# Delta-rule block inverses on 64 by 64 quarters of TensorE, and the sequences' states on column tiles and halves of rows

## The chip, the core and the metric

The kernel runs on one core of a Trainium2 chip. The metric is the device time of one execution in microseconds, taken as the median of the runs shown. One execution was taken by the hardware profiler; its trace is what the rows further down are read from. The engines are TensorE (PE; its weight loads are listed as PEld), VectorE (DVE), ScalarE (ACT), GpSimd (POOL) and SyncE (SP), which issues most DMAs.

## What is computed

One inference step of a two-layer decoder trunk: a gated delta-rule layer, then a sparse-attention layer, each followed by a convolutional feed-forward block. There are 512 new prompt tokens and 8 decoding sequences of 4 tokens each, width 1024. The change touches only the delta rule's core of the first layer. In the reference, cut to what matters (8 heads, key and value width 128):

```python
decay = jnp.exp(jnp.where(tril, G[..., :, None] - G[..., None, :], NEG))
kk = jnp.einsum('bhncd,bhnsd->bhncs', k, k)
A = jnp.where(strict, beta[..., :, None] * kk * decay, 0.0)
T = lax.linalg.triangular_solve(eye + A, eye, left_side=True, lower=True, unit_diagonal=True)
u_v = T @ (v * beta[..., None])
w_k = T @ (k * (beta * jnp.exp(G))[..., None])
def step(S, xs):                      # over the chunks of a sequence
    u = uvc - wkc @ S
    o = (qc * jnp.exp(Gc)[..., None]) @ S + qkc @ u
    S = S * jnp.exp(glc)[..., None, None] + jnp.einsum('bhcd,bhce->bhde', kdc, u)
    return S, o
```

The prompt is worked on in chunks; for each the inverse of a unit triangular matrix is wanted. The decoding sequences bring their own states S, two heads times eight sequences in a group.

## The kernel before

The kernel is written against a scheduling layer: each engine's instructions are put in order by the layer from the program's order and its own estimate of when operands are there, and tiles are recycled from pools with a fixed number of buffers. `gdn_core` holds the section of the change. It mixes generators: `run` takes several streams with a weight each, and `attend` always advances the stream that is furthest behind by its weight, so the `yield` values of a stream set how its operations are interleaved with the others'.

The prompt's eight heads go in two halves of four, `B[0]` and `B[1]`, over four chunks of 128 tokens: `gdn_blocks` (the matrix `na` per head, 128 by 512: four chunks side by side), `gdn_small` (the inverses of 16 by 16 diagonal blocks, on VectorE), `gdn_prep`, `gdn_inverse` (16 by 16 blocks merged to 32, 64 and 128), `gdn_scan` (the chunks in order, with the state) and `gdn_result`. The decode groups run beside them, four calls of `gdn_decode` cut into slices by `part(n)`.

`gdn_inverse` starts from Y, the block-diagonal inverses laid out by GpSimd (line 833). For each level it does three steps for each of the four heads of a half: four 128x128 transposes of Y into PSUM (line 840) and ScalarE's copy to X (line 841); four 128x128 matmuls of `na` and Y (line 847) and VectorE's product with the level's mask into R (line 849); four matmuls of X and R (line 857) and VectorE's subtraction from Y (line 858). All work on full 128-wide chunks at each level, and the mask leaves only the blocks of that level.

`gdn_decode` has, in its order: transposes and small matmuls for the group's 64 tokens (lines 938 to 989, most on 64x64), sixteen accumulated 128x128 matmuls of the spread keys and queries `zk` with the sixteen states (line 1001), the update u (line 1008) and the output (line 1013), and the new states: for each of four quarters of the states GpSimd spreads u (line 1033), a matmul with 64 rows of `kd` and 512 columns (line 1037), and VectorE's addition to the state (line 1039). `S0` is one buffer, so a group's states are loaded after the group before has stored its own.

The mask tile `cm` is loaded by a DMA that ScalarE issues at the head of the section (line 657); GpSimd clears `zk` after it in program order (line 658).

## Time and profile before

| what | value |
|---|---|
| median of three runs | 2026.49 us (2019.98 to 2029.86) |
| profiled execution, its own time | 2023.65 us |
| its span, first to last instruction | 2022.0 us |
| busy TensorE, share of the span | 1913.4 us, 95% |
| busy VectorE, ScalarE, GpSimd | 1138.1, 793.0, 602.6 us |
| mean granted TensorE clock | 0.966 of full |
| the section of the change | about 215 to 430 us from the span's start |

In a row of a timeline "x16" means sixteen consecutive instructions put together, and its length reaches from the first one's start to the last one's end; consecutive rows of TensorE overlap, since its instructions are pipelined. "128*128 128x128" is the shape of the stationary tile (rows by columns) and of the moving operand. A float32 matmul stands as two instructions (passes), a transpose as one. The name list is output, then inputs. "[0.20 <-PE ps L857]" tells how long the engine was idle before the row and what ended the wait.

### The profile page before, as it was taken

What the parts mean: (1) busy time and instruction counts of PE and PEld (TensorE: products, weight loads), DVE (VectorE), ACT (ScalarE), POOL (GpSimd) and SP (SyncE); (2) the same over time, 40 slices, a digit from 0 to 9 for tenths busy, and PEclk for the clock granted to TensorE, in tenths of its full rate; (3) what the DMA queues carried; (4) which work ended last, traced back from release to release, by engine and by line L of the source; (5) the groups of instructions that cost most, each with busy time, mean ns of one, the idle gap of its engine ahead of it and who ended that gap; (6) DMA issues with size and microseconds to landing.
All of it is one profiled execution on the core that took longest, in us unless ns stands there. A gap on an engine that the chain in (4) does not pass through costs nothing.

```text
span 2022.0 us, 42933 instructions
## 1 busy us (share of the span) xinstructions
PE 1913.4 (95%) x16796; PEld 1756.5 (87%) x16796; DVE 1138.1 (56%) x2215; ACT 793.0 (39%) x1517; POOL 602.6 (30%) x1164
## 2 busy tenths in 40 slices
PE   7999999989999999989989697999997999999997
PEld 7999878879999999989978374676776999999997
DVE  6675586665755655553330024676665476564654
ACT  5543335443433333342210003665754443342335
POOL 2332445112423322301334211233332243241321
PEclk9999989989999999999999787999998999999999
DMA  5222012142222232265578637687576222223221
GB/s 166 87 89 87 11 45 62 42 143 91 80 90 87 84 97 83 76 188 159 170 218 246 190 118 238 193 251 216 171 220 133 91 85 85 84 86 103 77 83 59
DMA packets 225647, 247.07 MB, mean 122 GB/s; under 512 B 29862, under 2 KB 181334, under 8 KB 225188
## 3 DMA queue, kind: packets, MB, share of 16 engines
q1 hardware_dynamic: 196564, 200.09, 32.7%
q10 hardware_dynamic: 19824, 24.72, 4.2%
q0 software_dynamic: 9056, 19.51, 3.3%
q8 instruction: 132, 2.16, 0.4%
q14 instruction: 71, 0.58, 0.1%
HBM read 211.38 MB, written 32.86 MB: 121 GB/s over the span
## 4 chain that ended last, share of the span: by engine, by line
PE 85%; DMA 6%; DVE 4%; ACT 2%; issue 1%; SPq 1%; POOL 0%; ACTq 0%; DVEq 0%; POOLq 0%
PE pdn L424 59%; PE ps L1523 6%; PE po L1825 2%; DMA kv<-in_cache_sel 1%; PE ps L1936 1%; PE pp L1805 1%; PE ps L1924 1%; PE pos L1995 1%; PE ps L847 1%; PE pp L1780 1%; PE ps L857 1%; DMA od<-od 1%; PE pq L1037 1%; PE pp L1781 1%; PE pq L1001 1%
## 5 line engine op out<-in xcount | busy, mean ns | idle before, releaser
L424 PE MATMUL pdn<-hh,whi 128*128 128x272 f32 (+1 forms) x2272 | 477.3, 291 | 3.1 <-ACT hh L323 2.3
L424 PE MATMUL pdn<-hh,wlo 128*128 128x272 f32 (+1 forms) x2272 | 472.1, 289 | 0.0
L424 PE MATMUL pdn<-hl,whi 128*128 128x272 f32 (+1 forms) x2272 | 470.1, 288 | 0.0
L397 ACT CAST whi<-wraw 128x1024 fp32r<-128x1024 f32 (+3 forms) x222 | 214.2, 966 | 454.1 <-PE pdn L424 393.4
L424 PEld LDWEIGHTS pdn<-hh,whi 128*128 128x128 f32 (+1 forms) x2272 | 357.4, 188 | 6.0 <-ACT hh L323 2.7
L424 PEld LDWEIGHTS pdn<-hl,whi 128*128 128x128 f32 (+1 forms) x2272 | 356.7, 188 | 0.7
L424 PEld LDWEIGHTS pdn<-hh,wlo 128*128 128x128 f32 (+1 forms) x2272 | 354.6, 188 | 1.1 <-issue 0.4
L398 DVE TENSOR_TENSOR wlo<-wraw,whi 128x1024 fp32r<-128x1024 f32 (+3 forms) x222 | 250.7, 1130 | 34.7 <-ACT whi L397 27.6
L1133 DVE SCALAR_TENSOR_TENSOR facc<-fext,par,facc 128x592 f32<-128x592 f32 x176 | 146.2, 831 | 19.5 <-ACT facc L1131 16.7
L453 DVE TENSOR_TENSOR xT<-pdn,xT 128x544 f32<-128x544 f32 x80 | 57.7, 724 | 163.9 <-PE pdn L424 163.9
L1126 POOL COPY fext<-fext 128x32 f32<-128x32 f32 x88 | 31.1, 353 | 393.1 <-DVE fext L1123 392.6
L424 PE MATMUL pdn<-gh,whi 128*128 128x272 f32 x704 | 146.3, 289 | 0.2
L424 PE MATMUL pdn<-gh,wlo 128*128 128x272 f32 x704 | 145.2, 288 | 0.3 <-DVE wlo L398 0.3
L424 PE MATMUL pdn<-gl,whi 128*128 128x272 f32 x704 | 144.9, 288 | 0.0
L1523 PE MATMUL ps<-x,wc 64*64 64x128 f32 (+1 forms) x2048 | 135.9, 401 | 7.9 <-DVE cT L1535 5.6
L1523 PEld LDWEIGHTS ps<-x,wc 64*64 64x64 f32 x2048 | 106.6, 155 | 37.1 <-issue 8.4
L1123 DVE TENSOR_TENSOR fext<-pdn,rstd 128x544 f32<-128x544 f32 x88 | 63.6, 725 | 114.0 <-PE pdn L424 113.3
L424 PEld LDWEIGHTS pdn<-gl,whi 128*128 128x128 f32 x704 | 110.0, 188 | 0.3 <-DVE gl L1147 0.2
L424 PEld LDWEIGHTS pdn<-gh,wlo 128*128 128x128 f32 x704 | 109.6, 188 | 0.8 <-DVE wlo L398 0.8
L424 PEld LDWEIGHTS pdn<-gh,whi 128*128 128x128 f32 x704 | 109.4, 188 | 0.8 <-ACT whi L397 0.7
L1790 POOL TENSOR_SCALAR e<-e,sm 128x128 f32<-128x128 f32 (+3 forms) x128 | 66.5, 540 | 110.1 <-DVE sm L1787 38.2
L1131 ACT ACTIVATE facc<-fext,par 128x592 f32<-128x592 f32 x88 | 77.6, 883 | 41.5 <-POOL fext L1126 41.4
(543 smaller groups left out, 3271.1 us busy)
## 6 DMA issues: line engine op xcount, KB each, us to landing
wraw<-in_ffn_w_up SPq DMA_DIRECT2D x40, 1024.0 KB
kv<-in_cache_sel SPq DMA_DIRECT2D x128, 256.0 KB
x<-in_cache_cmp SPq DMA_DIRECT2D x128, 128.0 KB
wraw<-in_gdn_w_in SPq DMA_DIRECT2D x15, 1024.0 KB
wraw<-in_ffn_w_down SPq DMA_DIRECT2D x16, 768.0 KB
x<-in_cache_cmp POOLq DMA_DIRECT2D x96, 128.0 KB, 3.4
wraw<-in_ffn_w_down SPq DMA_DIRECT2D x16, 640.0 KB
kv<-in_state_win SPq DMA_DIRECT2D x16, 512.0 KB
```

The costliest lines, as they stand in the source:

```text
L397: nc.scalar.copy(h, raw)
L398: nc.vector.tensor_tensor(l, raw, h.bitcast(F32), op=OP.subtract)
L424: nc.tensor.matmul(p[:mw, j, :TH], w[:, k, :mw], (x[k] if type(x) is list else x[:, k, :])[:, j * TH:(j + 1) * TH], start=k == 0 and n == ...
L453: self.nc.vector.tensor_tensor(self.two(self.xT[:, m, :]), p, self.two(self.xT[:, m, :]), op=OP.add)
L847: nc.tensor.matmul(p[:, s], B['na'][h][:, s], Y[h][:, s], start=True, stop=True)
L1123: nc.vector.tensor_tensor(self.two(ext[:, 2:2 + T]), p, self.two(rstd), op=OP.mult)
L1126: nc.gpsimd.tensor_copy(se[:, :, 2:6], ext[:, 514:546].rearrange("p (b j) -> p b j", j=4))
L1131: nc.scalar.activation(acc, ext[:, 0:592], AF.Identity, scale=ws[0], bias=self.pcol(f'ffn_b{i}', ft))
L1133: nc.vector.scalar_tensor_tensor(acc, ext[:, j:592 + j], ws[j], acc, op0=OP.mult, op1=OP.add)
L1523: nc.tensor.matmul(p[par][half(f), :n], W[c][half(par), d, :], x[half(par), :n, d], start=k == 0, stop=k == 31)
L1790: nc.gpsimd.tensor_scalar(ee, ee, sm[:, qt:qt + 1], 1.0, op0=OP.mult, op1=OP.mult)
L1825: nc.tensor.matmul(po[:, kt * 128:], vw, part[:, poff[kt]:poff[kt] + w], start=br == 0 and kt == 0 and part is ph, stop=br == 1 and kt == ...
```

## The change

In `gdn_inverse` the levels 16 and 32 work on the two diagonal 64 by 64 quarters of each chunk: the transposes become matmuls by the 64 by 64 identity, each matmul takes 64 rows and 64 columns, the two quarters write the upper and the lower 64 partitions of one PSUM tile of 256 columns, and the masks come from a new tile `cq` that GpSimd copies from `cm` at the head of the section. At level 64 only one quarter is computed: X of the upper quarter, `na` of the lower-left rows, and the result is written (negated) into the quarter of Y that was zero. In `gdn_decode` line 1001 becomes 32 matmuls on column tiles of 32, each with only the 32 columns of `zk` that its output rows need; `kd` is copied to the lower 64 rows as well, and the new states are computed in pairs on the upper and lower 64 rows with a PSUM tile each.

```diff
--- before.py
+++ after.py
@@ -655,6 +655,12 @@
             nc.scalar.preload_act_table_set("natural_log_exp_and_others")
         self.cmask = gs.tile([128, CM.shape[1]], F32, name="cm", bufs=1)
         nc.scalar.dma_start(self.cmask, A['c_m'])
+
+        G['cq'] = gs.tile([128, 2, 64], F32, name="cq", bufs=1)
+        for i, size in enumerate((16, 32)):
+            for j in range(2):
+                h = slice(j * 64, j * 64 + 64)
+                nc.gpsimd.tensor_copy(G['cq'][h, i, :], self.cm(size)[h, h])
         nc.gpsimd.memset(G['zk'], 0.0)
 
         idr = G['idr'] = gs.tile([128, 128], F32R, name="idr", bufs=1)
@@ -832,30 +838,47 @@
             X[h] = gs.tile([128, 512], F32, name="X", bufs=4)
             nc.gpsimd.tensor_tensor(Y[h].rearrange("p (c b e) -> p c b e", c=4, b=8), B['yc'][h][:, :, None, :].to_broadcast(bk),
                                     self.cm('blk')[:, None, :, None].to_broadcast(bk), op=OP.mult)
+        half = lambda j: slice(j * 64, j * 64 + 64)
+        own = lambda t, j, c: t[half(j), c * 128 + j * 64:c * 128 + j * 64 + 64]
+        v = lambda t: t.rearrange("p (c n) -> p c n", n=64)
+
         for size in (16, 32, 64):
+            both = range(2) if size < 64 else range(1)
+            rows = slice(0, 64 * len(both))
             for h in B['hs']:
                 p = self.ps()
                 for c in range(4):
-                    s = slice(c * 128, (c + 1) * 128)
-                    nc.tensor.transpose(p[:, s], Y[h][:, s], self.ident)
-                nc.scalar.copy(X[h], p)
+                    for j in both:
+                        nc.tensor.matmul(p[half(j), c * 64:(c + 1) * 64], own(Y[h], j, c), self.ident[half(j), half(j)], start=True, stop=True)
+                nc.scalar.copy(X[h][rows, 0:256], p[rows, 0:256])
                 yield 0.45
             for h in B['hs']:
                 p = self.ps()
                 for c in range(4):
-                    s = slice(c * 128, (c + 1) * 128)
-                    nc.tensor.matmul(p[:, s], B['na'][h][:, s], Y[h][:, s], start=True, stop=True)
+                    for j in both:
+                        k = j if size < 64 else 1
+                        na = B['na'][h][half(k), c * 128 + j * 64:c * 128 + j * 64 + 64]
+                        nc.tensor.matmul(p[half(j), c * 64:(c + 1) * 64], na, own(Y[h], k, c), start=True, stop=True)
                 R = B['R', h] = G['ge'].tile([128, 512], F32, name="dm", bufs=4)
-                nc.vector.tensor_tensor(R.rearrange("p (c n) -> p c n", c=4), p.rearrange("p (c n) -> p c n", c=4),
-                                        self.cm(size)[:, None, :].to_broadcast([128, 4, 128]), op=OP.mult)
+                if size < 64:
+                    nc.vector.tensor_tensor(v(R[:, 0:256]), v(p[:, 0:256]), G['cq'][:, size // 32, None, :].to_broadcast([128, 4, 64]), op=OP.mult)
+                else:
+                    nc.vector.tensor_copy(R[rows, 0:256], p[rows, 0:256])
                 yield 0.9
             for h in B['hs']:
                 p = self.ps()
                 R = B.pop(('R', h))
                 for c in range(4):
-                    s = slice(c * 128, (c + 1) * 128)
-                    nc.tensor.matmul(p[:, s], X[h][:, s], R[:, s], start=True, stop=True)
-                nc.vector.tensor_tensor(Y[h], Y[h], p, op=OP.subtract)
+                    for j in both:
+                        s = slice(c * 64, (c + 1) * 64)
+                        nc.tensor.matmul(p[half(j), s], X[h][half(j), s], R[half(j), s], start=True, stop=True)
+                yv = Y[h].rearrange("p (c n) -> p c n", c=4)
+                if size < 64:
+                    for j in both:
+                        y = yv[half(j), :, half(j)]
+                        nc.vector.tensor_tensor(y, y, v(p[half(j), 0:256]), op=OP.subtract)
+                else:
+                    nc.vector.tensor_scalar(yv[rows, :, half(1)], v(p[rows, 0:256]), -1.0, None, op0=OP.mult)
                 yield 0.9
 
     def gdn_scan(self, B):
@@ -948,9 +971,10 @@
         nc.vector.tensor_tensor(sc[:, 0:1], rk, G['gbd'][:, 1, hp:hp + 1], op=OP.mult)
         nc.vector.tensor_tensor(sc[:, 1:2], rk, sc[:, 0:1], op=OP.mult)
         nc.vector.scalar_tensor_tensor(sc[:, 2:3], sc[:, 1:2], -1.0, eG, op0=OP.mult, op1=OP.mult)
-        kd = gs.tile([64, 128], F32, name="dkd")
+        kd = gs.tile([128, 128], F32, name="dkd")
         rvb = gs.tile([64, 128], F32, name="drvb")
-        nc.scalar.activation(kd, p[:64, 0:128], AF.Copy, scale=eR)
+        nc.scalar.activation(kd[:64], p[:64, 0:128], AF.Copy, scale=eR)
+        nc.scalar.copy(kd[64:], kd[:64])
         nc.scalar.activation(rvb, p[:64, 256:384], AF.Copy, scale=sc[:, 0:1])
         wg = gs.tile([64, 64], F32, name="dwg")
         nc.gpsimd.tensor_scalar(wg, self.c('d_after', 64), G['gbd'][:, 0, hp:hp + 1], 1.0, op0=OP.mult, op1=OP.mult)
@@ -997,8 +1021,12 @@
                 nc.gpsimd.tensor_copy(dst, smp(G[nm][2 * hp + i]))
         yield 1.0
         p = self.pq.tile([128, 512], F32, name="pq")
-        for n in range(16):
-            nc.tensor.matmul(p[:, 0:128], zk[:, n, :], S0[:, n // 8, n % 8, :], start=n == 0, stop=n == 15)
+
+        for b in range(8):
+            for j in range(2):
+                for i in range(2):
+                    r = slice(j * 64 + i * 32, j * 64 + i * 32 + 32)
+                    nc.tensor.matmul(p[r, 0:128], zk[:, i * 8 + b, r], S0[:, i, b, :], start=b == 0, stop=b == 7)
         rr = gs.tile([64, 128], F32, name="drr")
         nc.vector.scalar_tensor_tensor(rr, p[:64, 0:128], sc[:, 2:3], rvb, op0=OP.mult, op1=OP.add)
         oq = gs.tile([64, 128], F32, name="doq")
@@ -1028,15 +1056,21 @@
         S0f = S0.rearrange("p i b n -> p (i b) n")
         eg = G['egl'][:, 2 * hp:2 * hp + 2, :].rearrange("p h b -> p (h b)")
         nc.gpsimd.tensor_tensor(S0f, S0f, eg[:, :, None].to_broadcast([128, 16, 128]), op=OP.mult)
-        for n in range(4):
-            um = G['ge'].tile([128, 512], F32, name="wg")[:64].rearrange("p (a n) -> p a n", a=4)
-            nc.gpsimd.tensor_tensor(um, u[:, None, :].to_broadcast([64, 4, 128]),
-                                    self.c('d_inst', 64)[:, 4 * n:4 * n + 4, None].to_broadcast([64, 4, 128]), op=OP.mult)
-            p = self.pq.tile([128, 512], F32, name="pq")
+
+        for n in (0, 2):
+            um = G['ge'].tile([128, 512], F32, name="wg").rearrange("p (a n) -> p a n", a=4)
+            ps = [self.pq.tile([128, 512], F32, name="pq") for _ in range(2)]
+            for j in range(2):
+                nc.gpsimd.tensor_tensor(um[j * 64:(j + 1) * 64], u[:, None, :].to_broadcast([64, 4, 128]),
+                                        self.c('d_inst', 64)[:, 4 * (n + j):4 * (n + j) + 4, None].to_broadcast([64, 4, 128]), op=OP.mult)
             yield 1.0
-            nc.tensor.matmul(p, kd, um.rearrange("p a n -> p (a n)"), start=True, stop=True)
-            v = S0f[:, 4 * n:4 * n + 4, :].rearrange("p a n -> p (a n)")
-            nc.vector.tensor_tensor(v, p, v, op=OP.add)
+            for j in range(2):
+                h = slice(j * 64, (j + 1) * 64)
+                nc.tensor.matmul(ps[j], kd[h], um[h].rearrange("p a n -> p (a n)"), start=True, stop=True)
+            for j in range(2):
+                v = S0f[:, 4 * (n + j):4 * (n + j) + 4, :].rearrange("p a n -> p (a n)")
+                nc.vector.tensor_tensor(v, ps[j], v, op=OP.add)
+            yield 1.0
         for i in range(2):
             nc.sync.dma_start(O['new_gdn_s'][0, :, 2 * hp + i].rearrange("b k v -> k b v"), S0[:, i])
```

## Rows read from the trace of the kernel before

**Rows 1.** The page: busy us of engines; granted clock in 40 slices, in tenths.

```profile
PE 1913.4 (95%) x16796; PEld 1756.5 (87%) x16796; DVE 1138.1 (56%) x2215; ACT 793.0 (39%) x1517; POOL 602.6 (30%) x1164
...
PEclk9999989989999999999999787999998999999999
```

**Rows 2.** The page: chain that ended last, shares by line.

```profile
PE pdn L424 59%; PE ps L1523 6%; PE po L1825 2%; DMA kv<-in_cache_sel 1%; PE ps L1936 1%; PE pp L1805 1%; PE ps L1924 1%; PE pos L1995 1%; PE ps L847 1%; PE pp L1780 1%; PE ps L857 1%; DMA od<-od 1%; PE pq L1037 1%; PE pp L1781 1%; PE pq L1001 1%
```

**Rows 3.** Windows: length, busy us of PE, PEld, DVE, ACT, POOL; granted clock; DMA.

```profile
290.00:295.00 5.00, 5.00 (x34) 3.72 (x32) 4.83 (x14) 0.00 (x0) 1.03 (x2) 1.00 0.40 108
...
390.00:395.00 5.00, 5.00 (x47) 5.00 (x46) 2.77 (x4) 0.59 (x1) 0.00 (x0) 1.00 0.00 0
```

**Rows 4.** Groups, TensorE, 265 to 400 us: count | busy us, mean ns.

```profile
L847 PE MATMUL ps<-Y,na 128*128 128x128 f32 x192 | 27.4, 300 | 0.0
L857 PE MATMUL ps<-dm,X 128*128 128x128 f32 x192 | 24.0, 278 | 1.3 <-DVE dm L849 1.3
L840 PE MATMUL ps<-cf,Y 128*128 128x128 f32 x96 | 14.1, 289 | 2.4 <-POOL Y L833 1.8 <-DVE ruk L308 0.7
L1037 PE MATMUL pq<-wg,dkd 64*128 64x512 f32 x24 | 12.8, 628 | 0.0
L1001 PE MATMUL pq<-S,zk 128*128 128x128 f32 x96 | 12.7, 278 | 0.0
```

**Rows 5.** Timeline, TensorE, second half of heads: start, length, what, count.

```profile
392.01 1.95 PE L847 MATMUL ps<-Y,na 128*128 128x128 f32 x16
393.80 0.39 PE L1001 MATMUL pq<-S,zk 128*128 128x128 f32 x2
394.02 1.95 PE L857 MATMUL ps<-dm,X 128*128 128x128 f32 x16
```

**Rows 6.** Timeline, VectorE, first half of heads, no idle before it.

```profile
283.73 0.68 DVE L858 TENSOR_TENSOR Y<-Y,ps 128x512 f32<-128x512 f32 x1
```

**Rows 7.** Timeline, VectorE, second half of heads, idle in brackets.

```profile
396.01 0.69 DVE L858 TENSOR_TENSOR Y<-Y,ps 128x512 f32<-128x512 f32 x1 [0.20 <-PE ps L857]
```

**Rows 8.** Groups, VectorE, 200 to 460 us.

```profile
L849 DVE TENSOR_TENSOR dm<-ps,cm 128x512 f32<-128x512 f32 x24 | 16.5, 687 | 7.6 <-PE ps L847 7.5
L858 DVE TENSOR_TENSOR Y<-Y,ps 128x512 f32<-128x512 f32 x24 | 16.4, 685 | 4.8 <-PE ps L857 4.8
...
L896 DVE COPY X<-ps 128x128 f32<-128x128 f32 x8 | 2.2, 280 | 0.0
```

**Rows 9.** Timeline, TensorE: passes on parts of the array.

```profile
384.10 0.33 PE L984 MATMUL pq<-dY,dna 64*64 64x64 f32 x2
...
1258.78 0.28 PE L1964 MATMUL ps<-mn,cf 64*64 64x1 f32 x4
...
1295.70 0.64 PE L1995 MATMUL pos<-kv,ptv 128*16 128x64 f32 x32
```

**Rows 10.** Window, line 1523 alone: length, PE busy (passes).

```profile
1076.00:1080.00 4.00, 4.00 (x72) 3.44 (x70) 1.00 0.79 228
```

**Rows 11.** Timeline, TensorE, where the tile shape changes twice.

```profile
400.73 0.39 PE L889 MATMUL ps<-u,kq 128*128 128x128 f32 x2
401.04 0.43 PE L1008 MATMUL pq<-drr,dY 64*64 64x128 f32 x2
401.40 0.49 PE L888 MATMUL ps<-u,kd 128*128 128x128 f32 x2
401.73 0.39 PE L889 MATMUL ps<-u,kq 128*128 128x128 f32 x2
```

**Rows 12.** Timeline, TensorE: decode steps within the scan.

```profile
310.57 3.84 PE L1001 MATMUL pq<-S,zk 128*128 128x128 f32 x32
...
323.60 1.93 PE L1037 MATMUL pq<-wg,dkd 64*128 64x512 f32 x4
```

**Rows 13.** Timeline, GpSimd and ScalarE, where the section starts.

```profile
231.47 1.05 POOL L706 TENSOR_TENSOR wg<-cg,g 128x512 f32<-128x512 f32 x1 [2.93 <-PE ps L714]
...
227.29 0.36 ACTq L657 DMA_DIRECT2D cm<-in_c_m  x1
```

## The prediction

> **What bounds the kernel now.** I read the page first, then windows of the delta-rule section, then its timelines. TensorE is busy for 95% of the span at full granted clock almost everywhere [rows 1], and the chain that ended last is mostly the dense line 424 at 59%; the lines of this change (847, 857, 1001, 1037) hold about 1% each [rows 2]. So the change can only move a small section, roughly 215 to 430 us, and what it saves there reaches the end one for one, since dense TensorE work follows.
>
> Inside the section two stretches matter. The block inverses of the first four heads (266 to 310 us) have VectorE as a second bound: 4.83 of 5 us busy in the window from 290 [rows 3], and a subtract that begins with no idle before it [rows 6]. The inverses of the other four heads (362 to 399 us) are pure TensorE: the window from 390 has TensorE at 5.00 and VectorE at 2.77 of 5 us [rows 3], sixteen passes follow each other every 0.112 us (393.80 less 392.01, over 16) [rows 5], and VectorE waits 0.20 us for TensorE before each operation [rows 7]. The reader should see there that a shorter matmul is worth its whole length in the second stretch, and in the first only until VectorE is full.
>
> **Inverses, TensorE.** The page counts a float32 matmul as two passes, a transpose as one: 96 + 192 + 192 passes over 24 head-levels [rows 4], so per head and level 4 transposes and 16 matmul passes, 20 x 0.112 = 2.23 us, 53.6 us in all. Afterwards the levels 16 and 32 have, in each of three steps, 4 chunks x 2 quarters x 2 passes = 16 passes (the transposes become matmuls by the identity and double); level 64 has 8 per step on one quarter. That is 16 x 48 + 8 x 24 = 960 passes on 64x64 quarters with 64 moving columns. The trace has no such stream. A pass with 128 columns takes 0.112 us, half the columns give 0.056 us (an estimate); line 984's two passes on one quarter take 0.33 us with their latency, which bounds a pass at 0.165 [rows 9].
>
> Do the two diagonal quarters run together? Line 1964 has two matmuls on opposite quarters, and its four passes are over in 0.28 us, less than the 0.33 us of line 984's two on one quarter [rows 9]: they overlap, though with one moving column. Four column tiles overlap plainly: line 1995 has 32 passes in 0.64 us, 0.020 us each where a lone pass of 64 columns would take 0.056 [rows 9]. The speaking row against is line 1523: four quarters, rows and columns both, 72 passes of 128 columns in 4 us, 0.0556 each, which is two at a time and not four [rows 10]. Two at a time is all that the diagonal asks. I take two at a time: 768/2 + 192 = 576 passes in turn, 32.3 us, 21.3 us less than 53.6. The ends are 0 (in turn, 960 x 0.056 = 53.8) and 21.3.
>
> **Inverses, VectorE.** An operation on 512 columns takes 0.687 us and on 128 columns 0.280 [rows 8]; between them 256 columns take 0.42. The mask product shrinks from 0.69 to 0.42; the subtract becomes two operations on half the rows, 0.84 for 0.69; at level 64 a copy and a negation, 0.42 each. Per four heads: 24 x 0.687 = 16.5 before, 8 x 1.26 + 4 x 0.84 = 13.4 after. So VectorE loses 3.1 us per stretch, and at levels 16 and 32 becomes as long as TensorE (1.26 against 1.34 per head), with the subtracts the slower side: 0.84 per head against 0.45 us of matmuls. What is late next in the second stretch is the next level's turn, waiting for the last head's subtract, 3 x 0.39 = 1.2 us per level.
>
> What remains of the gain: first stretch 6 us (low end 3.1, VectorE's own saving; high end 9, nearly all TensorE time). Second stretch, TensorE -10.7, less about 1.2 at two level changes, gives 9 (6 to 11). ScalarE's copies of X halve; ScalarE works 0.59 of 5 us in the second stretch [rows 3], so they and the decode's added copy cost nothing while that idle time is there, and some 0.3 us apiece without it.
>
> **Line 1001.** Sixteen 128x128 matmuls (32 passes, 3.84 us in the scan [rows 12], of which 32 x 0.112 = 3.6 are the passes' steps) become 32 on column tiles of 32, four of which run together. Four together with 128 columns take one pass's 0.112, 64/4 x 0.112 = 1.8 us. That saves 1.8 us in each of four decode groups. In one of them it stands ahead of the scan's first matmuls and counts in full; one lies in the second stretch; two lie beside other waits, 0.5 each. Against it stand changes of tile shape: from a 128x128 pass to line 1008's quarter and back costs 401.04 - 400.73 - 0.22 = 0.09 us on the way in, 401.40 - 401.04 - 0.22 = 0.14 on the way out and 401.73 - 401.40 - 0.22 = 0.11 for the first load [rows 11], 0.34 us in all. In the second stretch line 1001 runs as filler in pieces (two passes at 393.80 [rows 5]); eight pieces would be 2.7 us. I take 1.8 + 1.8 + 1.0 - 2.6 = 2 (-1.5 to 6). Within the inverses the decode's quarter-size steps stop changing the shape and its 128-wide ones start to; I count that as even.
>
> **Line 1037.** Four 64-row matmuls per group, 0.93 us for two passes (1.93 for four [rows 12]), become two pairs on halves of rows with separate PSUM tiles. If a pair overlaps, 1.7 us per group and 7 in all; if not, 0. The nearest row is line 1523, where rows and columns together gave two of four [rows 10], and columns alone could be the whole of it; I take 2. The Trainium skill, "TensorE: Matmul & The Clock Gate", section "Measured speedup vs the span model", gives 3.07 times for four row tiles; by it this term would be 7 and the time 5 us lower. No run here shows a pair of row tiles at 512 columns.
>
> **Small parts.** ScalarE copies kd to the lower rows once per group (in that same idle time), and GpSimd builds two masks' products ahead of a pair instead of one: GpSimd's count stays at 16, the number of yields too, so the interleaving plan keeps its shares. Four GpSimd copies of the mask wait for a load that ScalarE issues at 227.29; GpSimd idles 2.93 us until 231.47 [rows 13], which hides them. Were they put ahead of line 706's first products, those would come some 4 us late. I take 0.
>
> **Sum.** 6 + 9 + 2 + 2 = 19 us off the profiled execution's 2023.65 (span 2022.0 and 1.65 around it): 2004.65. The median of the runs, 2026.49, stands 2.84 above that execution, so I predict 2007 for the median. Bounds for this case: savings of 3.1 + 6 - 1.5 = 8 and 9 + 11 + 6 + 7 = 33, that is 1993 to 2019.
>
> **Rivals.** First, the quarters take turns because they write one PSUM tile. Then TensorE's inverses need 53.8 us, nothing won; at levels 16 and 32 they are longer (2.7 against 2.23 per head) and at 64 shorter; VectorE's 3 us in the first stretch and 2 from line 1001 are left at best, 0 to 5: 2024 to 2026 on the median's scale, no change. For it: line 1523's two of four. Against it: line 1964's 0.28 us. The Trainium skill, "TensorEngine Tiling (Array Packing)", section "Restrictions and Gotchas", says that different row tiles cannot access the same PSUM bank at once; by that rule this rival is what happens, and line 1964, the one pair of that kind in the trace, doesn't bear it out.
>
> Second, on the other side: they take turns and each turn also shows its weight load. The balance of 960 passes in turn is zero at 0.056 us a pass and tips at any more, 9.6 us per 10 ns. Line 1008 shows 0.36 us from its start to the next engine step for two passes with 0.22 of streaming [rows 11], 0.07 per pass exposed; half of that hidden by the other quarter leaves 0.09 a pass, 960 x 0.034 = 33 us more: about 2057.
>
> Third, the matmuls do shrink but VectorE and shape changes eat the gain: the first stretch gives 3, the second 6, lines 1001 and 1037 nothing: 8 us, 2018.
>
> **How the numbers follow.** The forecast case has 0.60, the turns without cost 0.20, the turns with exposed loads 0.10, the eaten gain 0.10. The range reaches from 1995 (most of the forecast's upper bound) to 2028 (the second case with a few late GpSimd microseconds); it leaves out the slow rival and the top of the savings. The runs shown spread over half a per cent, about what a measurement can tell from no change; half a per cent is 10 us, so faster means under 2016. The forecast gives 0.55 of its 0.60 there, the eaten gain 0.03: 0.58. No change: 0.05 + 0.06 + 0.18 = 0.29. Slower: 0.13.
>
> **What would show it.** Lines 840, 847 and 857 (by their new numbers) should hold 320 passes each in quarters, with a head's sixteen passes done in 0.45 us; 0.9 us means turns, more means loads exposed. In the second stretch VectorE should stand near 4 of 5 us and its idle before the subtracts vanish. Line 1001's 64 passes should take under 2 us, in few pieces. A pair on line 1037 should start within a few ns of each other and be over in 0.9 us rather than 1.8. The prediction is wrong if the stretch from 362 us keeps its 36 us, or if GpSimd's first product moves behind the mask's load.

## The result, and the profile after

The changed kernel takes 2041.56 us (median of five; 2041.12 to 2044.42), the kernel before 2023.87 (five runs, among them the three reported above): 1.0095 times as long, 95% interval 1.0071 to 1.012. The forecast was 2007, with 1995 to 2028 as its range. The profiled execution of after has a span of 2039.5 us.

The page of after, its busy line and its clock in 40 slices:

```profile
PE 1900.8 (93%) x17404; PEld 1739.6 (85%) x17404; DVE 1136.5 (56%) x2231; ACT 791.1 (39%) x1521; POOL 601.6 (29%) x1168
...
PEclk9999977989999999998998698999998999999999
```

TensorE is busy 12.6 us less than before and the span is 17.5 us longer [rows 1]; the sixth and seventh slice (255 to 357 us, the section) now show 7. Groups of after on TensorE, 265 to 440 us (for [rows 4]), then its timeline (start, length, count, idle before in brackets):

```profile
L852 PE MATMUL ps<-cf,Y 64*64 64x64 f32 x320 | 18.0, 250 | 10.3 <-POOL Y L839 6.4 <-DVE Y L879 3.4 <-DVE kq L825 0.4
L1069 PE MATMUL pq<-wg,dkd 64*128 64x512 f32 x32 | 17.9, 875 | 0.0
L874 PE MATMUL ps<-dm,X 64*64 64x64 f32 x320 | 17.1, 239 | 3.1 <-DVE dm L866 1.6 <-DVE dm L864 1.3
L861 PE MATMUL ps<-Y,na 64*64 64x64 f32 x320 | 14.6, 236 | 1.2 <-ACT X L853 1.2
L1029 PE MATMUL pq<-S,zk 128*32 128x128 f32 x192 | 9.7, 278 | 0.0
```

```profile
275.61 1.12 PE L852 MATMUL ps<-cf,Y 64*64 64x64 f32 x16 [6.39 <-POOL Y L839]
...
287.49 3.88 PE L1069 MATMUL pq<-wg,dkd 64*128 64x512 f32 x6
...
311.85 1.95 PE L1029 MATMUL pq<-S,zk 128*32 128x128 f32 x64
...
322.89 0.37 PE L1051 MATMUL pq<-cf,do 64*128 64x64 f32 x1 [1.41 <-POOL do L1048]
322.90 2.17 PE L1069 MATMUL pq<-wg,dkd 64*128 64x512 f32 x4
...
386.98 2.03 PE L861 MATMUL ps<-Y,na 64*64 64x64 f32 x64
388.85 2.03 PE L874 MATMUL ps<-dm,X 64*64 64x64 f32 x64
...
401.95 1.21 PE L861 MATMUL ps<-Y,na 64*64 64x64 f32 x18
...
434.92 2.23 PE L1069 MATMUL pq<-wg,dkd 64*128 64x512 f32 x8
```

Lines 852, 861 and 874 are the old 840, 847 and 857; 1029 is the old 1001, 1069 the old 1037. The matmuls do what was forecast: 64 passes in 2.03 us, two quarters at a time, where sixteen took 1.95 [rows 5]; at level 64, where one quarter works alone, 18 passes in 1.21; 64 passes of the sum in 1.95, four at a time; eight passes of the updates in 2.23, two at a time, where four took 1.93 [rows 12]. The loss is in the idle brackets, and in the length that one line has in two places: six passes of line 1069 take 3.88 us at 287, eight take 2.23 at 434. Windows of after (length, busy us of PE, PEld, DVE, ACT, POOL, then the granted clock as a share of 2.4 GHz):

```profile
275.00:280.00 5.00, 4.39 (x83) 4.39 (x85) 3.39 (x13) 1.38 (x4) 5.00 (x6) 0.57 0.10 12
290.00:295.00 5.00, 5.00 (x25) 1.97 (x24) 2.50 (x13) 0.00 (x0) 0.00 (x0) 0.50 0.11 28
...
325.00:330.00 5.00, 5.00 (x12) 2.70 (x12) 2.30 (x4) 0.80 (x3) 1.05 (x1) 0.50 0.37 105
385.00:390.00 5.00, 4.65 (x159) 4.51 (x156) 4.19 (x9) 1.49 (x4) 0.78 (x1) 1.00 0.38 105
395.00:400.00 5.00, 4.87 (x146) 4.76 (x144) 4.76 (x12) 0.37 (x1) 0.00 (x0) 1.00 0.40 107
```

At 290 the clock was 1.00 before [rows 3] and is 0.50 now, the lower of its two levels (1.2 of 2.4 GHz).

I cut the section by TensorE's timeline: the first inverse from its first transpose to the scan's first product, the second likewise, and the start of the output projection on line 424, behind which all kernels do the same work. All times in the table are from one profiled execution each; median and ratio are of the runs.

| kernel | first inverse from, for | second inverse for | line 424 from | median | ratio, interval |
|---|---|---|---|---|---|
| before | 266.6, 42.9 | 35.7 | 431.3 | 2023.87 | |
| after | 275.6, 49.8 | 23.4 | 449.1 | 2041.56 | 1.0095, 1.0071 to 1.012 |
| e1 copies alone | 275.8, 43.2 | 35.7 | 443.5 | 2032.15 | 1.0045, 1.0025 to 1.0065 |
| e2 quarters, masks as constants | 269.1, 50.0 | 23.1 | 435.2 | 2022.18 | 0.9989, 0.9971 to 1.0007 |
| e3 sequences' part alone | 272.2, 39.6 | 36.8 | 433.2 | 2022.57 | 1.0006, 0.9989 to 1.0023 |
| e4 whole change, masks as constants | 272.2, 47.9 | 23.3 | 444.1 | 2035.74 | 1.0063, 1.0039 to 1.0087 |
| e5 quarters, heads 4 to 7 only | 268.5, 41.7 | 23.0 | 424.0 | 2017.17 | 0.9974, 0.9955 to 0.9994 |
| e6 e5 and sequences' part | 269.4, 41.0 | 22.4 | 424.6 | 2018.06 | 0.9974, 0.9955 to 0.9993 |
| e7 e2, first half's products twice | 268.9, 64.5 | 23.1 | 446.0 | 2036.81 | 1.0091, 1.0058 to 1.0124 |
| e8 e2 and the sum | 271.9, 45.1 | 23.0 | 435.7 | 2028.75 | 1.0021, 1.0001 to 1.0042 |
| e9 e2, fillers in the first half | 269.6, 68.7 | 23.1 | 450.4 | 2040.09 | 1.0086, 1.006 to 1.0113 |
| e10 e2, sequences' steps moved | 269.2, 42.2 | 24.7 | 430.6 | 2019.28 | 1.0006, 0.998 to 1.0031 |
| e11 e4, one step to ScalarE | 272.1, 46.6 | 23.3 | 444.6 | 2035.37 | 1.0068, 1.0046 to 1.0089 |
| e12 e6, one step to ScalarE | 271.4, 42.8 | 22.6 | 434.5 | 2025.79 | 1.0014, 0.9998 to 1.0031 |
| e13 e2, first half's transposes whole | 266.5, 39.1 | 23.0 | 423.1 | 2008.80 | 0.9933, 0.9913 to 0.9954 |
| e14 e4, sequences' steps moved | 272.0, 39.2 | 27.4 | 433.5 | 2028.88 | 1.0023, 1.001 to 1.0037 |
| e15 e5, last step of heads 0 to 3 on quarters | 266.2, 37.6 | 23.0 | 420.4 | 2013.90 | 0.9945, 0.9926 to 0.9965 |
| e16 e13 and sequences' part | 269.6, 42.3 | 23.3 | 431.2 | 2020.56 | 0.9988, 0.9974 to 1.0001 |
| e17 e13 and the sum | 271.7, 44.8 | 23.0 | 431.8 | 2021.94 | 0.998, 0.9964 to 0.9997 |
| e18 e17, first pair's sum as before | 269.3, 39.2 | 23.0 | 423.1 | 2016.66 | 0.9979, 0.9964 to 0.9994 |

From line 424 to the end the kernels take 1581.7 (e13) to 1594.6 us (e15) in these executions, 1590.7 before and 1590.4 after. The runs don't tell why, so steps are judged by the column "line 424 from", and the median says what is left of it. One of e1's ten runs took 7274.27 us, in a slow state, and is left out of its ratio.

How far does one execution stand for its kernel? e2 and e13 have the same instructions in the same order up to the first inverse, and e2's inverse begins 2.6 us later: e2 is 1.0 us late at 216 us already, and near 250 us its clock falls where that of e13 doesn't. The windows from 250 to 254 of e2, then of e13:

```profile
250.00:254.00 4.00, 3.70 (x17) 3.25 (x18) 1.52 (x11) 2.08 (x8) 0.81 (x1) 0.57 0.00 0
```

```profile
250.00:254.00 4.00, 4.00 (x35) 3.59 (x33) 3.04 (x14) 2.24 (x7) 2.09 (x2) 1.00 0.02 4
```

So the granted clock, too, can differ between executions of the same instructions, and a difference of up to some 3 us between two rows isn't read as an effect. In 15 of the 19 changed kernels the interval of the ratio (of 2022 us) holds what the column gives; in e2, e13, e17 and e18 it misses it, by 0.9 to 2.5 us.

Between before and after the section loses 17.8 us: the first inverse starts 9.0 later, takes 6.8 more, 6.3 more lie between it and the second inverse, the second takes 12.3 less, and 7.9 more lie behind it (rounded).

### The profile page after: what moved, and what is told of

The parts are those of the page before. It is cut to its first block, busy times and chain, and to the rows that moved or that the text cites. A ratio compares the mean times of both kernels' runs of the same rounds, so it can differ in the third digit from the quotient of the medians.

```text
span 2039.5 us, 44196 instructions
## 1 busy us (share of the span) xinstructions
PE 1900.8 (93%) x17404; PEld 1739.6 (85%) x17404; DVE 1136.5 (56%) x2231; ACT 791.1 (39%) x1521; POOL 601.6 (29%) x1168
## 4 chain that ended last, share of the span: by engine, by line
PE 79%; DMA 5%; DVE 5%; issue 4%; ACT 2%; POOL 1%; POOLq 1%; SPq 1%; ACTq 1%; DVEq 0%
PE pdn L424 58%; PE ps L1557 3%; PE po L1859 1%; PE ps L1958 1%; PE ps L1970 1%; PE pos L2029 1%; PE pp L1814 1%; PE pp L1839 1%; POOLq L1500 1%; DMA qd<-qrotd 1%; PE pp L1815 1%; DMA od<-od 1%; POOL x L1501 1%; DMA kv<-in_cache_sel 1%; DMA cgate<-in_c_n 1%
## 5 line engine op out<-in xcount | busy, mean ns | idle before, releaser
L398 DVE TENSOR_TENSOR wlo<-wraw,whi 128x1024 fp32r<-128x1024 f32 (+3 forms) x222 | 249.8, 1127 | 35.3 <-ACT whi L397 22.6
```

The source lines that it names most:

```text
L398: nc.vector.tensor_tensor(l, raw, h.bitcast(F32), op=OP.subtract)
```

## The experiments

**The parts by themselves.** My theories after the result: A, the mask copies change the order ahead of the inverse; B, quarters let TensorE's clock fall; C, the sequences' part costs.

e1 adds the copies to the kernel before; nothing reads them.

```diff
+        G['cq'] = gs.tile([128, 2, 64], F32, name="cq", bufs=1)
...
+                nc.gpsimd.tensor_copy(G['cq'][h, i, :], self.cm(size)[h, h])
```

> The kernel before with only the four GpSimd copies of the masks added; nothing reads them, every inverse stays full width. Theory A (the copies cost a wait of their own: they stand ahead of line 706's products on GpSimd's queue and wait for the masks' load, and the scheduler takes another order on VectorE and TensorE from there on, so the first inverse starts 9.0 us later, 275.6 instead of 266.6 in the trace): 2029 to 2034, ratio 1.003 to 1.005, with the first inverse's first matmul at about 275. Rival B (the quarters themselves leave TensorE idle and its clock falls to 0.50): no difference here, 2022 to 2026. Rival C (the sequences' part costs): no difference here either.

2032.15, as A has it, and line 424 begins 12.2 us later. GpSimd in after, then in e1 (idle in brackets):

```profile
230.35 1.06 POOL L663 COPY cq<-cm 64x64 f32<-64x64 f32 x4 [1.49 <-DMA cm<-in_c_m]
231.85 1.05 POOL L712 TENSOR_TENSOR wg<-cg,g 128x512 f32<-128x512 f32 x1 [0.44 <-PE ps L720]
```

```profile
231.06 1.05 POOL L663 COPY cq<-cm 64x64 f32<-64x64 f32 x4 [1.51 <-DMA cm<-in_c_m]
232.56 1.05 POOL L712 TENSOR_TENSOR wg<-cg,g 128x512 f32<-128x512 f32 x1 [0.45 <-PE ps L720]
...
274.70 4.09 POOL L839 TENSOR_TENSOR Y<-yc,cm 128x512 f32<-128x512 f32 x4 [6.94 <-DMA yc<-dt]
```

The first product moves by 0.38 us only (231.85 for 231.47 [rows 13]). What moves is the order behind it. VectorE in before, then in after:

```profile
234.85 3.19 DVE L752 SCALAR_TENSOR_TENSOR na<-pq,sc,dm 128x128 f32<-128x128 f32 x12
...
244.29 1.04 DVE L757 TENSOR_REDUCE dg<-dm 128x64 f32<-128x512 f32 x1
...
249.25 0.16 DVE L777 TENSOR_TENSOR itmp<-tt,inst 128x1 f32<-128x1 f32 x1
```

```profile
235.23 2.15 DVE L758 SCALAR_TENSOR_TENSOR na<-pq,sc,dm 128x128 f32<-128x128 f32 x8
...
238.50 0.29 DVE L743 CUSTOM_DVE_ANT_0 jk<-pq,cf 128x128 bf16<-128x128 f32 x1 [1.11 <-PE pq L740]
...
249.47 1.01 DVE L763 TENSOR_REDUCE dg<-dm 128x64 f32<-128x512 f32 x1
...
254.51 0.87 DVE L783 TENSOR_TENSOR itmp<-tt,inst 128x1 f32<-128x1 f32 x1 [1.17 <-DMA inst<-dn]
```

Twelve products in a row became eight, then a wait for TensorE; the fourth reduction comes 5.2 us later, and with it the first of the fifteen steps of the small inverses, on which the first block inverse waits. e1 has the same wait and order, so the copies alone do it.

e2 is the inverses without the copies: the quarters' masks take the place of the mask of step 64 among the constants.

```diff
-                    (64, ((j // 64) % 2 == 0) & (s // 64 == j // 64 + 1)),
+                    ('cq', own),
...
+        cq = self.cm('cq').rearrange("p (i n) -> p i n", i=2)
```

> Only the inverses of the change, on quarters; their masks come with the constants (the unused mask of step 64 gives its columns to them), so no copies run and nothing ahead of the inverse moves; the sequences' part stays as before. Theory A: the first inverse starts at 266.6 as before, and my sum of 15 us for both inverses comes out in large part: 2008 to 2016, ratio 0.992 to 0.996. Rival B (idle TensorE and clock at 0.50 in the first half's inverse and the scans take it back): 2024 to 2032, with windows at a granted clock of 0.50 between 265 and 320. Rival C (the sequences' part costs 8 to 17 us): 2008 to 2016 here, and the loss stands in the run of that part alone.

2022.18, a little under B's range and far from A's: the second inverse wins 12.6 us, the first loses 7.1. e3 is the diff from `kd` on, with the inverses as before:

> Only the sequences' part of the change: the sum over states on column tiles of 32, the updates on halves of rows, the copy of the scaled keys; the inverses stay full width and no mask is copied. Theory A and rival B: my sum for these two, 4 us, or nothing: 2018 to 2026, ratio 0.997 to 1.001. Rival C (the sequences' part costs, by its copy on ScalarE, its later updates and GpSimd's scaling of the states): 2030 to 2040.

2022.57: C falls, and so does my 4 us. e4 is the whole change with e2's constants:

> The whole change, with the quarters' masks among the constants in place of the four copies: nothing else differs from the changed kernel. Theory A: at least the 9 us ahead of the inverse come back, 2026 to 2034, and where the order was also behind the first inverse's clock, down to 2008. Rival B: 2036 to 2042, as with the copies. Rival C: 2034 to 2042.

2035.74: some of the copies' cost comes back, but e2 and e3, nothing each, are 13 together. That is in C's range, though C had e3 lose, and just outside A's and B's.

**Which half, and which part.** e5 puts a condition on the half, and e6 adds the sequences' part:

```diff
+        if B['i'] == 0:
+            for size in (16, 32, 64):
...
+            return
         for size in (16, 32, 64):
             both = range(2) if size < 64 else range(1)
```

> The inverses on quarters for heads 4 to 7 only, full width for heads 0 to 3; masks among the constants; the sequences' part as before. In the run with quarters in both halves and the sequences' part as before, the second inverse took 23.1 us instead of 35.7 and the first 50.0 instead of 43.0, with TensorE granted 0.50 from 270 to 305. Theory B (the first stretch loses because TensorE waits there for other engines and its clock goes to 0.50): the first stretch comes back to 43 us, the second keeps its 12: the outputs' products start at 418 to 424 instead of 431.3, 2008 to 2014, ratio 0.993 to 0.996. Rival D (what the second inverse gains is given back in the scan behind it, because the sequences' steps that lay beside the inverse then lie in the scan; 33.3 us from the inverse's end to the outputs before, 37.7 with quarters): 2017 to 2022.

> As the run with quarters for heads 4 to 7 only, with the sequences' part of the change added. Theory B alone: as that run, to 3 us less: 2006 to 2014. Rival D with the sequences' part (the two together lengthen the second scan: 41.4 us from the inverse's end to the outputs in the run of the whole change with constant masks, 31.8 with the sequences' part alone): 2020 to 2026.

2017.17 lies in D's range, above B's. The first inverse is back at 41.7, the second keeps 23.0, line 424 begins 7.3 us earlier than before: less than 12.7, since 38.0 us follow the second inverse where 33.3 did. That is rival D's part, and the traces show it: before has 43 passes of the sequences (counted by their lines) beside the second inverse (9.6 us of TensorE) and 23 behind it (6.6), e5 has 13 (4.5) and 53 (10.9). With the sequences' part added, 2018.06 lies between the two forecasts and nothing changes, so that part costs only beside quarters in the first half. e8 is e2 with the sum alone:

> Quarters in both halves with the masks among the constants, and of the sequences' part only the sum over states on column tiles of 32; the updates stay whole. The inverses alone gave 2022.2, with the whole sequences' part 2035.7. Theory F (the earlier sum releases GpSimd's scaling of the states before the last step of the small inverses; that step then took 3.30 us instead of 0.40, and the first inverse started at 272.2): at least half of the 13.5 us are here: 2029 to 2036. Rival G (the updates on halves of rows, two products behind two GpSimd steps, cost in the scans): 2020 to 2025 here.

2028.75 lies just under F's range. By the medians 6.6 of the 13.6 us come with the sum and 7.0 with the updates; by line 424 it is 0.4 and 8.4, so the sum's share is not settled here.

**What lengthens the first inverse.** Windows of e2:

```profile
275.00:280.00 5.00, 4.71 (x74) 4.52 (x74) 5.00 (x15) 0.60 (x2) 4.94 (x5) 0.50 0.02 2
285.00:290.00 5.00, 5.00 (x29) 2.34 (x28) 2.53 (x7) 0.00 (x0) 2.07 (x2) 0.50 0.11 28
290.00:295.00 5.00, 5.00 (x19) 1.87 (x20) 4.61 (x20) 0.37 (x1) 0.00 (x0) 0.50 0.06 19
300.00:305.00 5.00, 2.01 (x33) 1.71 (x31) 3.56 (x17) 1.55 (x6) 0.00 (x0) 0.50 0.45 134
```

From 284.7 to 300.3 its TensorE has no gap, at 0.50. At 1.00 the same would take half at best, an estimate of up to 7.8 us less; the stretch is 7.1 too long. Is the clock the cause, or a companion of waits? e7 and e9 give TensorE more to do, with the other engines' work unchanged; e10 takes the sequences' 16 steps away.

```diff
+        again = [c for c in range(4) for _ in range(2 if B['i'] == 0 else 1)]
...
-                for c in range(4):
+                for c in again:
```

> As the run with quarters in both halves and the sequences' part as before (2022.2), with every product of the first half's inverse issued twice (the second writes the same result over the first), so that TensorE has 640 passes there instead of 320 and the other engines the same work. Theory B (clock): TensorE is granted 1.00 for more of 270 to 305, the first inverse takes 42 to 47 us instead of 50.0 although TensorE does twice the passes; 2014 to 2020. Rival E (VectorE's and GpSimd's own work sets that stretch, the clock follows it): 49 to 52 us, granted clock or not, 2021 to 2025. Were TensorE's passes the bound, 320 more at 0.028 us a pass would add 9 us: 2031.

```diff
+                nc.tensor.matmul(p.rearrange("p (c n) -> p c n", c=4), G['idr'], G['no_upto'][:, None, :].to_broadcast([128, 4, 128]), start=True, stop=True)
```

> As the run with quarters in both halves and the sequences' part as before (2022.2), with one product of 128 by 512 of constants put ahead of every group of quarters of the first half's inverse (36 of them, 0.32 to 0.48 us each at full clock), into the same buffer, which the group then overwrites: TensorE has something to run where it would wait for the group's operands, and the other engines have the same work. Theory B (TensorE's waits let its clock fall to 0.50 and the stretch pays for that): granted 1.00 in most of 265 to 310, the first inverse takes 42 to 47 us instead of 50.0 in spite of 12 us of extra products; 2014 to 2020. Rival H (the sequences' steps between the quarters on TensorE's queue wait for other engines, and the clock only follows): 50 to 56 us, 2022 to 2030.

Both missed every number: 64.5 and 68.7 us. In e7 TensorE waits in its queue for a sequences' step that GpSimd scales (its timeline, first), and e9's windows, second:

```profile
285.47 0.37 PE L1045 MATMUL pq<-cf,do 64*128 64x64 f32 x1 [4.36 <-POOL do L1042]
```

```profile
290.00:295.00 5.00, 5.00 (x27) 2.52 (x26) 3.68 (x17) 0.37 (x1) 2.06 (x2) 0.50 0.07 24
305.00:310.00 5.00, 5.00 (x52) 3.49 (x51) 1.29 (x5) 0.05 (x1) 0.00 (x0) 0.50 0.61 129
315.00:320.00 5.00, 5.00 (x44) 4.28 (x44) 1.97 (x6) 0.00 (x0) 0.00 (x0) 0.50 0.01 3
```

In e9 TensorE was busy for all of 290 to 320 and stayed at 0.50, so much of the extra work was paid at half rate. That speaks against B as I had put it, since having work did not bring 1.00 back; apart from that, neither run tells clock from waits.

```diff
-        n = (11, 16, 6, 6, 5, 0)
+        n = (11, 0, 22, 6, 5, 0)
```

> As the run with quarters in both halves and the sequences' part as before (2022.2), with the 16 steps of the sequences that lay beside the first inverse given to the scan behind it (shares 11, 0, 22, 6, 5, 0 instead of 11, 16, 6, 6, 5, 0). Rival H (the quarters wait on TensorE's queue behind the sequences' steps): the first inverse falls from 50.0 to 32 to 40 us; the scan behind it gets longer by 4 to 10. Theory B: the inverse still takes 45 or more, at 0.50. Rival E (VectorE's own work, with the other half's small inverses, sets the stretch): 43 to 50 us. For the whole: 2016 to 2026.

42.2 us, between the forecasts of H and of E, and still at 0.50 from 275 to 295. The steps between the quarters are a part of the loss, but without them quarters are no shorter than full width with them (e5, 41.7), and line 424 begins at 430.6, 0.8 us earlier than before. e13 changes one step in e2: the first half's transposes are 128 wide again, as real transposes of one pass, ScalarE's copies of them 512 wide, and the third step reads X from its diagonal quarters. VectorE's work stays that of quarters.

```diff
+                if B['i'] == 0:
+                    for c in range(4):
+                        s = slice(c * 128, (c + 1) * 128)
+                        nc.tensor.transpose(p[:, s], Y[h][:, s], self.ident)
+                    nc.scalar.copy(X[h], p)
...
```

> As the run with quarters in both halves and the sequences' part as before (2022.2), with the first half's transposes at full width (48 passes of 128 by 128 in place of 160 of 64 by 64, ScalarE's copies 512 wide instead of 256); products, masks and subtractions stay on quarters. Theory B (the granted clock): 1.00 in most of 270 to 310, as with full width, and the first inverse takes 40 to 44 us instead of 50.0: 2012 to 2018. Theory E and H (VectorE's queue and the sequences' steps): 47 to 52 us with the clock at either level: 2020 to 2026.

2008.80, ratio 0.9933, the fastest of all. The first inverse takes 39.1 us. Windows of e13, then the same four updates in e2 and in e13:

```profile
275.00:280.00 5.00, 3.47 (x61) 3.31 (x60) 5.00 (x13) 0.90 (x4) 3.58 (x4) 0.50 0.13 13
...
285.00:290.00 5.00, 5.00 (x57) 2.85 (x56) 3.90 (x14) 0.70 (x2) 2.03 (x2) 1.00 0.06 20
290.00:295.00 5.00, 3.96 (x61) 2.49 (x60) 4.83 (x18) 1.14 (x6) 1.96 (x9) 1.00 0.39 105
...
300.00:305.00 5.00, 4.50 (x69) 4.08 (x68) 4.79 (x19) 1.19 (x3) 0.00 (x0) 1.00 0.81 216
```

```profile
284.71 3.73 PE L1058 MATMUL pq<-wg,dkd 64*128 64x512 f32 x4
```

```profile
284.61 1.93 PE L1065 MATMUL pq<-wg,dkd 64*128 64x512 f32 x4
```

TensorE is busy less than in e9 and has 1.00 from 285 to 335, and VectorE, at 4.8 of 5 us from 290 to 305, is the bound of the stretch. The stretch is 10.9 us shorter than in e2, but not by the clock alone, since the two don't hold the same work. From the first transpose to the scan's first product, e2 has 64 passes of the sequences, 17.4 us of TensorE; e13 has 26 in 7.5, before 26 in 7.4. The eight update passes among them take 7.87 us in e2 and 4.18 in e13: that is the clock. The second pair's sum takes 3.84 us in both, but the layer's order puts it ahead of the scan's first product in e2 (309.30, the scan from 319.13) and behind it in e13 (306.98, the scan from 305.64), with six small passes:

```profile
309.30 3.84 PE L1022 MATMUL pq<-S,zk 128*128 128x128 f32 x32
```

```profile
305.64 1.16 PE L910 MATMUL ps<-v,Y 128*128 128x128 f32 x8
...
306.98 3.84 PE L1029 MATMUL pq<-S,zk 128*128 128x128 f32 x32
```

Up to line 424 e13 is 12.2 us ahead of e2, of which 2.6 stand ahead of the first inverse. That the edit pays is shown by the ratios too (0.9933 for 0.9989); how the gain divides between the clock and the order isn't. e15 is e5 with quarters in the last step of the first half, where they add no second subtraction:

```diff
-            for size in (16, 32, 64):
+            for size in (16, 32):
...
-            return
-        for size in (16, 32, 64):
+        for size in (64,) if B['i'] == 0 else (16, 32, 64):
```

> As the run with quarters for heads 4 to 7 only (2017.2, ratio 0.9974), with the first half's last step, the one of 64, on quarters too: per head a copy of 256 and a negation of 256 (0.41 us each) in place of a mask and a subtraction of 512 (0.68 each), and 48 passes of 64 in place of 48 of 128. If the gain of quarters holds where nothing is added for VectorE: the first inverse takes 40 to 42 us instead of 42 to 43, 2013 to 2017. If the clock falls to 0.50 behind it: 2018 to 2022.

37.6 us, shorter than forecast and the shortest first inverse of all, at 1.00 in every window from 265 to 335, as in e5, which needs 41.7; line 424 from 420.4, 10.9 us earlier than before; 2013.90, inside the first range.

**Why the sequences' part costs beside quarters.** In after, line 1051 stands ahead of the first inverse's last passes and waits for a step that GpSimd's queue holds behind four products. e11 and e12 move that step to ScalarE, in e4 and e6:

```diff
-        nc.gpsimd.tensor_scalar(o, o, ro, 1.0, op0=OP.mult, op1=OP.mult)
+        nc.scalar.activation(o, o, AF.Copy, scale=ro)
```

> As the whole change with the masks among the constants (2035.7), with the sequences' output scaled by ScalarE instead of GpSimd. On GpSimd that step stood behind the four products of 1.08 us for the updates, TensorE's transpose of it stood ahead of the first inverse's last passes and waited 1.74 us at 318.2, and the scan behind ran at a granted clock of 0.50 from 320 to 330. Theory I (that queue is what the updates on halves cost beside quarters): 2026 to 2031, with the wait gone and the scan at 1.00. Otherwise 2033 to 2038.

> Quarters for heads 4 to 7 only, the whole sequences' part, and the sequences' output scaled by ScalarE. The run without the last step gave 2018.1, ratio 0.9974. If the step behind GpSimd's four products holds TensorE in the second scan too (40.6 us from the second inverse's end to the outputs against 33.3 before): 2012 to 2016, ratio 0.994 to 0.997; if not, 2016 to 2020.

2035.37: the wait falls from 1.74 to 0.65 us, but the next window still has 0.50, and theory I falls. e12, at 2025.79, lies above both forecasts and 7.7 us above e6, by a longer stretch between the inverses (56.6 us for 51.2) that no run explains. Timeline and window of e11:

```profile
317.26 0.27 PE L1049 MATMUL pq<-cf,do 64*128 64x64 f32 x1 [0.65 <-ACT do L1046]
```

```profile
320.00:325.00 5.00, 5.00 (x10) 1.78 (x9) 1.11 (x3) 0.53 (x2) 0.27 (x1) 0.50 0.39 105
```

e14 is e4 with e10's shares:

> The whole change with the masks among the constants (2035.7), with the sequences' 16 steps moved from beside the first inverse to the scan behind it, as in the run that gave 2019.3 without the sequences' part. Theory H (their place between the quarters is what makes the two parts of the change cost together): 2018 to 2026. Otherwise (the sum released early, the updates on halves themselves): 2032 to 2038.

2028.88, between the two forecasts: the place of these steps is about half of it. Then e16 and e17, e13 with the whole sequences' part and with the sum alone:

> The run with full-width transposes in the first half and quarters elsewhere (2008.8, ratio 0.9933), with the whole sequences' part of the change added. If the granted clock is what made the two parts cost together (13.5 us beside quarters in both halves): 2006 to 2012, since the first stretch is at 1.00. If the order of the queues does it by itself (the sum released before the small inverses' last step, the updates ahead of the first scan): 2016 to 2024.

> As that run (2008.8) with the sum over states on column tiles alone added. If the clock made the parts cost together: 2006 to 2010. If the earlier release of GpSimd's scaling costs by itself (the last step of the small inverses 3.30 us instead of 0.40, the first inverse from 272 on instead of 266.5): 2012 to 2018.

2020.56, in the range of the theory of the queues, and 2021.94, above both forecasts: beside e13 the sum alone does it all. VectorE and GpSimd in e13, then in e17:

```profile
260.34 0.40 DVE L780 TENSOR_TENSOR itmp<-tt,inst 128x225 f32<-128x225 f32 x1
...
261.12 3.61 POOL L1058 TENSOR_TENSOR S<-S,egl 128x2048 f32<-128x2048 f32 x1 [1.44 <-PE pq L1029]
```

```profile
261.87 3.84 POOL L1062 TENSOR_TENSOR S<-S,egl 128x2048 f32<-128x2048 f32 x1
...
262.66 3.29 DVE L780 TENSOR_TENSOR itmp<-tt,inst 128x225 f32<-128x225 f32 x1
```

Against VectorE's chain GpSimd's scaling of the states, which waits for the sum, starts 1.6 us sooner (0.79 us ahead of the last multiply of the small inverses, where it was 0.78 behind it), and that multiply, 0.40 us alone, ends 0.24 us behind the scaling. The Trainium skill, "SBUF — State Buffer", section "SBUF: two separate sides", says that a GpSimd instruction that reads SBUF and a VectorE operation with two inputs in SBUF use one port pair, and that whichever starts first holds it for its whole instruction. The traces agree: the multiply takes 3.29 or 3.30 us in the nine kernels where the scaling starts ahead of it (e3, e4, e6, e8, e11, e12, e14, e16, e17) and 0.39 or 0.40 in the other eleven. After is one of the eleven: its chain on VectorE is so late that the scaling is over before the multiply begins. In e17 the first inverse begins at 271.7; TensorE idles meanwhile, and runs at 0.50 from 270 to 280 and from 285 to 295. e18 leaves the first pair's sum as before:

```diff
+        if hp == 0:
+            for n in range(16):
+                nc.tensor.matmul(p[:, 0:128], zk[:, n, :], S0[:, n // 8, n % 8, :], start=n == 0, stop=n == 15)
-        for b in range(8):
+        for b in range(8) if hp else ():
```

> The run with full-width transposes in the first half and quarters elsewhere (2008.8, ratio 0.9933), with the sum over states on column tiles for the second, third and fourth pair of heads, and as before for the first pair, whose sum lies beside the last steps of the small inverses. If the early release of GpSimd's scaling by the first pair's sum is what the sum costs (2021.9 with all four pairs on column tiles): 2004 to 2011, the first inverse from about 266.5 on, as without the sum's change. If the sums of the later pairs cost too, in the scans: 2014 to 2022.

The multiply takes 0.40 us again, and line 424 begins at 423.1, as in e13 and 8.7 us before e17: 2.4 of them ahead of the first inverse, 5.6 in it. Both executions have the fall of the clock near 250, and e13 hasn't. So by the traces it is the first pair's place alone. The medians don't bear that out: 2016.66 is in the other theory's range, and e18's ratio is that of e17 (0.9979 and 0.998). What a later sum of the first pair is worth at the end is not shown. In full-width e3 the same late start, 272.2, was made good in the inverse (39.6 us), which is why the sum looked free there.

## Why the prediction was wrong, step by step

**Inverses, TensorE.** Right: 320 passes on each line, 0.029 us a pass (388.85 less 386.98, over 64; the forecast had 0.45 over 16), two quarters at a time, in one PSUM tile. So both rivals with turns fell. Alone, at level 64, a quarter's pass takes 0.058 (1.21 less 0.22, over 17), twice that. The Trainium skill, "TensorEngine Tiling (Array Packing)", section "Restrictions and Gotchas", says that different row tiles cannot access one PSUM bank at the same time. Here quarters on different rows, and on different columns too, write two halves of the partitions of one PSUM tile two at a time, and the measurement decides.

**Second stretch.** I took 9 us; it gave 12.3, more than my upper end of 11, with VectorE at 4.19 and 4.76 of 5 us in two of its windows as forecast. Not in my sum: part of it is work that left the stretch. In e5 30 passes of the sequences went from beside the inverse to behind it (5.1 us less there, 4.3 more behind), and of 12.7 us 4.7 are lost again. The 8.0 that remain are near the 9.

**First stretch.** The step that failed. I took 6 us off; it grew by 6.8 (7.1 in e2). I had priced each pass at the clock of before, asked only when VectorE is full, and taken the stretch to hold the same work. My low end, VectorE's saving of 3.1, is near what the stretch gives where clock and work are nearly those of before (3.8 in e13). In after it isn't so: TensorE waits 6.9 us for VectorE and 3.5 for GpSimd (2.2 and 1.8 before), the clock is 0.50 in much of the stretch, and the layer's order puts 101 passes of the sequences there, 15.6 us of TensorE, in place of 26 in 7.4 (e2: 64 in 17.4); 64 of the 101 are the second pair's sum, 1.95 us. That the clock falls and that the work moves is shown; how much each of them costs, and why the clock stays low in one execution and not in another, is open.

**Line 1001.** I took 2 us. 64 passes in 1.95 us is the 1.8 forecast; the gain is none. e18, with three of the four sums on column tiles, reaches line 424 when e13 does, and the fourth releases GpSimd's scaling early (8.7 us at line 424, e17 against e18). In after that collision isn't there, since the copies have made VectorE's chain late already.

**Line 1037.** I took 2. The pairs do overlap (eight passes in 2.23 us), which would have been my 7, and nothing of it is seen at line 424: e16 and e17 differ by 0.6 us at line 424, and beside quarters in both halves the updates cost 8.4 (e4 against e8). Why that much there is open: in e4 the clock is 0.50 from 320 to 330 and in e8 1.00, and e11 excludes one queue as the reason.

**Small parts.** I took 0 for the copies and named the move of GpSimd's first product as what would prove me wrong. That move was 0.38 us; the cost at line 424 was 12.2 us in e1, by the order that the layer then gave to VectorE and TensorE, and 5.0 in company of the rest (after against e4). This is the second step that failed: a term that I put at nothing because the copies fit into idle time. I had said that the interleaving plan keeps its shares: the shares are kept, the order isn't.

My rivals all kept the order and the clock of before; what they gave was 2018 to 2026 and 2057, and none of them describes this loss. At line 424 the forecast and the result are 36.8 us apart: the first stretch is 12.8 of them, its late start 9.0, the stretches behind the two inverses, which my sum left out, 6.3 and 7.9, lines 1001 and 1037 4.0, and the second stretch takes 3.3 back (rounded). With clock and work nearly those of before (e13), line 424 begins 8.2 us earlier, where the inverses' terms had 15: the inverses win 3.8 and 12.7, and the stretches behind them give back 3.9 and 4.5. That e13's median, 2008.80, is near the forecast of 2007 is in part luck: its profiled execution gains another 9.0 us behind line 424, where nothing was changed, and my sum reached 19 with 4 us from lines that gave nothing.

## What to carry to other kernels

Where another engine sets a stretch, a shorter matmul mostly makes TensorE wait, and the work behind may run at half clock, as in e2. Shorten it where TensorE sets the pace (e5) or where the other engine's work shrinks with it (e15); in e13 wide transposes in between went with the better clock. Count a stretch together with the one behind it, since a layer that orders the queues moves other work between them. An instruction added "in a gap" must be priced by the order of the queues behind it, which is to be looked up, not assumed; constants that need no instruction are safer. When an operation gets faster, ask what it releases, and on which engine that collides.

## What the hardware showed

- TensorE, busy 5.00 of 5 us in every window from 290 to 320 (e9), stayed at 0.50 for 30 us; with 128-wide transposes in the same stretch it had 1.00 at 3.03 to 5.00 us busy (e13, 285 to 305).
- With the same instructions up to there, TensorE was granted 0.57 from 250 to 254 in one profiled execution (e2) and 1.00 in another (e13).
- Two 64 by 64 quarters on different rows and columns run together into one PSUM tile: 0.029 us a pass, where one quarter alone takes 0.058 (after).
- A multiply of 225 columns on VectorE, both inputs in SBUF, took 3.29 us instead of 0.40 when GpSimd's scaling of 2048 columns had begun before it (e17, e13).
- Two products on opposite halves of rows with 512 columns run together: eight passes in 2.23 us (after), where four in turn took 1.93 [rows 12].
